# Three phase boundaries: four blocks' weights made ahead, the statistics in another PSUM bank, the first half's row factors and outputs handled inside the next group of products

## The chip, the cores and the metric

The kernel runs on one core of one Trainium2 chip. Its time is device microseconds (us) of that core; every time below is from profiles and timed runs of this kernel on such a chip. Four engines do the work and have a queue each, in which they go through their instructions in order: PE (TensorE, matrix products, with its weight loads listed apart as PEld), DVE (VectorE), ACT (ScalarE) and POOL (GpSimd). SP (SyncE) issues the loads from HBM.

## The reference

A sequence of 512 tokens of width 1024 goes through two layers, and each is a mixing part and a feed-forward part (FFN). All parts have the same frame:

```
h = h + rmsnorm(part(rmsnorm(h, pre gain)), post gain)
```

- Layer A mixes by a gated MLP (chunks of 128 tokens, six groups) beside attention to a memory of 256 rows.
- Layer B mixes by causal attention with forget gates (12 heads) beside the same kind of memory attention.
- FFN: `down(silu(x @ w_gate) * (x @ w_up))` with 2816 hidden columns, which are 22 blocks of 128.

Everything is fp32. A normalization needs, for each token, the sum of the squares of its 1024 values, that is across the whole width.

## The kernel before

**Numbers.** Each fp32 operand is split into a high part and a rest (`split`, L241): ACT writes the high part, rounded to the matrix engine's type fp32r, and DVE subtracts it from the operand to get the rest. In the profile these are `whi` and `wlo` for weights, `xshi` and `xslo` for inputs, `fhi` and `flo` for the FFN's hidden values. A product is three matmuls (`mm3`): hi by hi (L193), rest of the input by hi (L194), hi by rest of the weight (L195). One weight block, 1024 x 128 values in a tile of 128 x 1024, takes two ACT casts and two DVE subtractions of 128x512 each.

**Layout.** The residual `h` lies transposed, width on the 128 partitions and tokens along the row; the last product of a part (`y`, "out" or "down") lies the other way, tokens on the partitions, in four blocks of 128 tokens.

**A boundary** between two parts (`boundary`, L875) is called three times: from layer A's mixing to its FFN (about 140 to 195 us), from that FFN to layer B (about 500 to 550 us), and from layer B's mixing to its FFN (about 727 to 785 us). `scaled` is given in the first and third and is `None` in the second. It goes so:

1. `tail(0)` to `tail(3)`: the last products of the part before, one block of 128 tokens each. DVE adds them up into `y` (L808), ACT sums the squares (L811), DVE and POOL make the row factor `r` (L813, L262), ACT scales `y` by it (L832).
2. In between, the first four weight blocks of the next part are prepared: `block(n, aside)` issues the load and the split. For the FFN the four are gate, up, gate, up. `aside` takes the two parts from another pool (the pool of the inputs, 36 buffers) than the weights' own pool of eight pairs. `behind(...)` sets the preparation behind the last split of `tail(0)`.
3. `turn(half, pairs)`: PE transposes `y` into a PSUM bank with the tag "tr" (`yt`, L839), DVE adds it to the residual `h` (L844), ACT scales by the gain of the next norm and the result is split into `xshi` and `xslo`; ACT squares `h` (L318) and DVE adds the squares up (L321, L323). The first half of the tokens is turned before the products, the second half inside them.
4. `group(ws, inputs(0), ...)`: the products of the four blocks with the first half of the tokens (256 columns), k from 0 to 7. The fourth block begins three steps later. What stands in `after` is put behind step k: the turns of the second half behind k=3 and k=5, the norm's `finish` behind k=6.
5. `finish` (L284 on): PE sums the squares across the partitions (`st`, four one-column matmuls of which each token block takes two, L290), DVE adds epsilon (`var`, L293), POOL takes the power -1/2 (`r`, L262). `spread`: PE spreads the factors `r` over the partitions (`rb`, two transposes, L259) and DVE copies them to `rbc` (L306). The products are of unnormalized inputs; the factors come in afterwards.
6. `evac`: in the FFN, gate times `rbc` (`gr`, L1070), silu on ACT (L1072), times up (`f`, L1074), and the split into `fhi` and `flo`. This frees the four banks of the first group.
7. The same four blocks with the second half, in two groups of two, then `finish` and later `spread` and `evac` for that half.

PSUM has eight banks here: three with the tag "mm", three "lg", two "tr". The first group holds two "mm" and two "lg"; "tr" serves the transposes `yt`, the statistics `st` and the spread rows `rb`.

**Order.** The program is written in the order above, but a scheduler at build time orders the instructions of each engine by priority (the order of the text, unless `high_priority` is set) and its own estimate of when their inputs are ready, and deals out the buffers of a pool in turn. So a change in the text moves instructions in other places too.

Of the kernel before, what the change touches and what calls it, by code (L numbers as in the profile page):

```python
# [15 lines left out]
P = 128  # L16
T = 512
D = 1024
KT = 8
# [21 lines left out]
def hybrid(ctx: ExitStack, tc: tile.TileContext, i: dict, out: bass.AP):  # L41
# [12 lines left out]
    def name(s):  # L54
        n_of[s] = n_of.get(s, 0) + 1
        return f"{s}_{n_of[s]}"

    def act(s, dt=F32R, shape=(P, T)):
        return ap.tile(list(shape), dt, tag="a", name=name(s))

    def plain(s, shape=(P, T), dt=F32):
        return yp.tile(list(shape), dt, tag="y", name=name(s))
# [7 lines left out]
    def small(s, n=4, dt=F32):  # L70
        return sp.tile([P, n], dt, tag=f"s{n}", name=name(s))

    def ps(tag, shape=(P, T), s="ps"):
        return pp.tile(list(shape), F32, tag=tag, name=name(s), bufs=2 if tag == "tr" else 3)
# [26 lines left out]
    def gain(block, k):  # L101
        c = block * KT + k
        return gains[:, c : c + 1]
# [87 lines left out]
    def mm3(o, w, x, start, stop, more=False):  # L191

        PE.matmul(o, w[0], x[0], start=start, stop=False, skip_group_check=more)  # L193
        PE.matmul(o, w[0], x[1], start=False, stop=False, skip_group_check=more)  # L194
        return PE.matmul(o, w[1], x[0], start=False, stop=stop, skip_group_check=more)  # L195

    def group(ws, xs, cols, tags, nk=KT, what="ps", after={}, lag=0):


        c0, c1 = cols  # L200
        outs = [ps(t, (P, c1 - c0), s=what) for t in tags]

        def step(b, k):
            mm3(outs[b], ws[b][k], (xs[k][0][:, c0:c1], xs[k][1][:, c0:c1]), k == 0, k == nk - 1)

        last = len(ws) - 1
        for k in range(nk):
            for b in range(last):
                step(b, k)
            for x in range(0 if k == lag else k, k + 1) if k >= lag else ():  # L210
                step(last, x)
            if k in after:
                after[k]()
        return outs
# [33 lines left out]
    @contextmanager  # L248
    def behind(some):

        with ExitStack() as s:
            for ins in some:
                s.enter_context(tc.issue_after(ins.ins))
            yield
# [6 lines left out]
    def rsqrt(dst, src, n):  # L261
        G.tensor_tensor(out=dst, in0=src, in1=mhalf[:, :n], op=ALU.pow)  # L262

    class Norm:
# [13 lines left out]
                A.activation(sq, src, AF.Square)  # L278
                V.tensor_add(self.acc, self.acc, sq)

        def finish(self, cols):

            c0, c1 = cols
            tbs = range(c0 // P, c1 // P)  # L284
            t0, t1 = c0 // P, c1 // P
            st = ps("tr", (P, 4), s="st")
            for tb in tbs:
                some = self.sums(tb, cols)
                for n, sq in enumerate(some):
                    PE.matmul(st[:, tb : tb + 1], sq, avg, start=n == 0, stop=n == len(some) - 1)  # L290
            v = small("var")
            with tc.high_priority():
                V.tensor_scalar_add(v[:, t0:t1], st[:, t0:t1], RMS_EPS)  # L293
                rsqrt(self.r4[:, t0:t1], v[:, t0:t1], t1 - t0)
# [37 lines left out]
    def normed_parts(block, k, cols, hi, lo):  # L332
        c0, c1 = cols
        scaled_parts(h[:, k, c0:c1], gain(block, k), hi[:, c0:c1], lo[:, c0:c1])

    def parts(s):
        return [(act(f"{s}hi"), act(f"{s}lo")) for _ in range(KT)]
# [498 lines left out]
    def turned(ys, k, tbs, out):  # L836

        for n, tb in enumerate(tbs):
            PE.transpose(out[:, n * P : (n + 1) * P], ys[tb][k // 4][:, k % 4 * P : (k % 4 + 1) * P], ident)  # L839

    def residual(o, k, cols, post):

        c0, c1 = cols
        V.scalar_tensor_tensor(out=h[:, k, c0:c1], in0=o, scalar=gain(post, k), in1=h[:, k, c0:c1],  # L844
                               op0=ALU.mult, op1=ALU.add)
# [29 lines left out]
    def boundary(phase, post, pre, nnorm, dst, block, evac, scaled=None):  # L875

        tail, ys = phase
        h0, h1 = HALVES
        xs = {} if scaled is not None else parts("xs")

        def turn(half, pairs):
            cols = HALVES[half]
            c0, c1 = cols
            for j in pairs:
                tr = ps("tr", s="yt")
                for x in range(2):  # L890
                    turned(ys, 2 * j + x, (2 * half, 2 * half + 1), tr[:, 256 * x : 256 * x + 256])
                for x in range(2):
                    residual(tr[:, 256 * x : 256 * x + 256], 2 * j + x, cols, post)
                    if scaled is None:
                        normed_parts(pre, 2 * j + x, cols, *xs[2 * j + x])
                if scaled is not None:
                    scaled[j, half] = plain("hs", (P, 2, 256))
                    for x in range(2):
                        A.activation(scaled[j, half][:, x, :], h[:, 2 * j + x, c0:c1], AF.Copy,
                                     scale=gain(pre, 2 * j + x))  # L900
                    xs[j, half] = pair_parts("xs", scaled[j, half])
                nnorm.pair(j, cols)

        def inputs(half):
            if scaled is not None:
                return [tuple(t[:, k % 2, :] for t in xs[k // 2, half]) for k in range(KT)]
            c0, c1 = HALVES[half]
            return [tuple(t[:, c0:c1] for t in xs[k]) for k in range(KT)]

        tail(0)  # L910
        phase_parts = tuple(last_parts)
        tail(1)
        with behind(phase_parts):
            ws = [block(n, n == 2) for n in range(3)]
        tail(2)
        turn(0, range(2))
        tail(3, lambda: turn(0, (2,)))
        turn(0, (3,))
        ws.append(block(3, False))
        outs = group(ws, inputs(0), h0, ["mm", "lg"] * 2, lag=3,  # L920
                     after={3: lambda: turn(1, range(2)), 5: lambda: turn(1, range(2, 4)),
                            6: lambda: nnorm.finish(h0)})
        nnorm.spread(h0, dst)
        evac(outs, h0)
        outs = group(ws[:2], inputs(1), h0, ["mm", "lg"])
        nnorm.finish(h1)
        outs += group(ws[2:], inputs(1), h0, ["mm", "lg"])

        def close():
            nnorm.spread(h1, dst)  # L930
            evac(outs, h1)

        return xs, close

    def pair_parts(s, src, room=None):

        hi, lo = room or [act(f"{s}{n}", shape=(P, 2, 256)) for n in ("hi", "lo")]
        split(src, hi, lo)
        return hi, lo
# [120 lines left out]
    def feed_forward(layer, phase, xp, meanwhile=None):  # L1060
# [39 lines left out]

        scaled = {}
        a, close = boundary(phase, G_MIX_POST + layer, G_FFN_PRE + layer, nnorm, rb, first, evac_first, scaled)
        w = [down_weights(layer, 0, dh) for dh in range(2)]
        close()
# [42 lines left out]
    def layer_b(phase, fp):  # L1147
# [16 lines left out]
        def evac_first(outs, cols):  # L1164
            for m, o in zip(first, outs):
                queries(m, o, cols)

        a, close = boundary(phase, G_FFN_POST, G_MIX_PRE + 1, bnorm, rbc,
                            lambda n, aside: prepared(i["w_b_q"][first[n]], (KT, P), aside), evac_first)
        for m in range(2, 6):  # L1170
# [176 lines left out]
    def give(tb, order, queues=(nc.sync,)):  # L1347

        c = (tb * P, (tb + 1) * P)
        for n, some in enumerate(order):  # L1350
            tr = ps("tr", s="yt")
            for x, k in enumerate(some):
                turned(ys, k, (tb,), tr[:, x * P : (x + 1) * P])
            for x, k in enumerate(some):
                residual(tr[:, x * P : (x + 1) * P], k, c, G_FFN_POST + 1)
            k0, k1 = some[0], some[-1] + 1
            queues[n % len(queues)].dma_start(out[:, k0:k1, c[0] : c[1]], h[:, k0:k1, c[0] : c[1]])
# [69 lines left out]
```

## Time and profile before

| | us |
|---|---|
| median of 3 runs | 1115.33 (1115.09 to 1115.86) |
| the profiled execution | 1114.41 |
| its span | 1112.7 |
| PE busy / PEld busy | 1103.1 / 1000.2 |
| DVE busy / ACT busy / POOL busy | 891.2 / 660.5 / 25.4 |

The profiled execution took 0.92 us less than the median. The clock granted to PE was 0.999 of full speed over the whole span. Matmuls are pipelined, and a matmul's end is modelled: one of 256 columns is listed with 0.28 us, while the next one begins about 0.12 us after its start. So PE appears busy in pauses that are shorter than this overlap, and a pause is better read from the starts of two neighbouring matmuls. DVE and ACT instructions are listed with their own ends, which lie a little behind the start of the next.

### The profile page before, as it was taken

The numbers are of one execution on the slowest core, as the hardware profiler recorded it, in microseconds if no ns is written. First come the engines' busy times: TensorE is split into PE (matmuls) and PEld (weight loads), VectorE is DVE, ScalarE is ACT, GpSimd is POOL, SyncE is SP. The second block draws the span as 40 slices with busy tenths as digits, with TensorE's granted clock in tenths as the row PEclk, the third lists the DMA queues.
The fourth block names the chain that finished last, engine by engine and source line by source line (L and its number), as shares of the span: only waits on it lengthen the run. The fifth ranks groups of instructions, "written<-read, shape, count | busy, mean of one in ns | idle before, by whom it ended". The sixth has DMA issues, their size and how long they took to land.

```text
span 1112.7 us, 19537 instructions
## 1 busy us (share of the span) xinstructions
PE 1103.1 (99%) x7409; PEld 1000.2 (90%) x7409; DVE 891.2 (80%) x1721; ACT 660.5 (59%) x1388; POOL 25.4 (2%) x41
## 2 busy tenths in 40 slices
PE   9999999999999999999999999999999999999998
PEld 6998889999899899998988888889999899899996
DVE  7879558998698588797968889858998598588776
ACT  7775468665265254477647667768665266255453
POOL 0000000000000000001000000000000000000000
PEclk9999999999999999999999999999999999999999
DMA  7522231334134233244232654431125234233222
GB/s 268 159 79 74 88 104 58 114 95 153 57 115 136 58 111 114 77 153 151 78 95 71 159 125 130 129 95 57 58 95 161 67 109 132 65 112 116 77 76 76
DMA packets 63557, 118.12 MB, mean 106 GB/s; under 512 B 5164, under 2 KB 39992, under 8 KB 63464
## 3 DMA queue, kind: packets, MB, share of 16 engines
q1 hardware_dynamic: 62584, 116.05, 34.5%
q8 instruction: 58, 0.95, 0.4%
q0 software_dynamic: 192, 0.52, 0.2%
q10 hardware_dynamic: 688, 0.31, 0.1%
q14 instruction: 35, 0.29, 0.1%
HBM read 104.71 MB, written 2.10 MB: 96 GB/s over the span
## 4 chain that ended last, share of the span: by engine, by line
PE 89%; DVE 5%; ACT 3%; issue 1%; DMA 1%; POOL 0%; SPq 0%; POOLq 0%; DVEq 0%; ACTq 0%
PE y L193 9%; PE y L195 9%; PE y L194 9%; PE a L195 5%; PE a L193 5%; PE a L194 5%; PE e L193 3%; PE e L195 3%; PE x L193 3%; PE x L195 3%; PE e L194 3%; PE x L194 3%; PE ps L195 3%; PE ps L193 3%; PE ps L194 3%; PE v L193 2%
## 5 line engine op out<-in xcount | busy, mean ns | idle before, releaser
L241 ACT CAST whi<-raw 128x512 fp32r<-128x512 f32 x460 | 276.1, 620 | 261.3 <-PE y L195 118.6
L241 DVE TENSOR_TENSOR wlo<-raw,whi 128x512 fp32r<-128x512 f32 x460 | 305.8, 685 | 112.4 <-ACT whi L241 110.0
L193 PE MATMUL y<-whi,fhi 128*128 128x512 f32 (+1 forms) x356 | 139.8, 393 | 0.0
L194 PE MATMUL y<-wlo,fhi 128*128 128x512 f32 (+1 forms) x356 | 139.3, 391 | 0.0
L195 PE MATMUL y<-whi,flo 128*128 128x512 f32 (+1 forms) x356 | 139.3, 391 | 0.0
L193 PE MATMUL x<-xshi,whi 128*128 128x256 f32 x320 | 89.7, 280 | 0.0
L195 PE MATMUL x<-xshi,wlo 128*128 128x256 f32 x320 | 89.7, 280 | 0.0
L195 PE MATMUL a<-xshi,wlo 128*128 128x256 f32 x320 | 89.6, 281 | 0.0
L193 PE MATMUL a<-xshi,whi 128*128 128x256 f32 x320 | 89.6, 280 | 0.0
L194 PE MATMUL x<-xslo,whi 128*128 128x256 f32 x320 | 89.6, 280 | 0.0
L194 PE MATMUL a<-xslo,whi 128*128 128x256 f32 x320 | 89.5, 280 | 0.0
L195 PEld LDWEIGHTS y<-whi,flo 128*128 128x128 f32 x356 | 66.9, 188 | 15.6 <-DVE flo L241 0.2
L193 PEld LDWEIGHTS y<-whi,fhi 128*128 128x128 f32 x356 | 66.8, 188 | 15.0 <-DVE y L808 0.2
L194 PEld LDWEIGHTS y<-wlo,fhi 128*128 128x128 f32 x356 | 66.9, 188 | 14.9 <-DVE wlo L241 0.2
L195 PE MATMUL ps<-xshi,wlo 128*128 128x256 f32 (+1 forms) x224 | 66.7, 299 | 1.3 <-DVE wlo L241 1.3
L193 PE MATMUL ps<-xshi,whi 128*128 128x256 f32 (+1 forms) x224 | 67.7, 303 | 0.0
L194 PE MATMUL ps<-xslo,whi 128*128 128x256 f32 (+1 forms) x224 | 66.5, 297 | 0.0
L194 PEld LDWEIGHTS a<-xslo,whi 128*128 128x128 f32 x320 | 60.3, 188 | 0.3
L193 PEld LDWEIGHTS a<-xshi,whi 128*128 128x128 f32 x320 | 60.3, 188 | 0.3
L195 PEld LDWEIGHTS x<-xshi,wlo 128*128 128x128 f32 x320 | 60.3, 189 | 0.0
L193 PEld LDWEIGHTS x<-xshi,whi 128*128 128x128 f32 x320 | 60.3, 188 | 0.0
L194 PEld LDWEIGHTS x<-xslo,whi 128*128 128x128 f32 x320 | 60.3, 188 | 0.0
(291 smaller groups left out, 3086.7 us busy)
## 6 DMA issues: line engine op xcount, KB each, us to landing
raw<-in_w_gate SPq DMA_DIRECT2D x44, 512.0 KB
raw<-in_w_up SPq DMA_DIRECT2D x44, 512.0 KB
raw<-in_w_down SPq DMA_DIRECT2D x44, 512.0 KB
raw<-in_w_out SPq DMA_DIRECT2D x16, 512.0 KB
raw<-in_w_b_q SPq DMA_DIRECT2D x8, 512.0 KB
raw<-in_w_a_v SPq DMA_DIRECT2D x6, 512.0 KB
raw<-in_w_a_u SPq DMA_DIRECT2D x6, 512.0 KB
raw<-in_w_v SPq DMA_DIRECT2D x6, 512.0 KB
```

The costliest lines, as they stand in the source:

```text
L193: PE.matmul(o, w[0], x[0], start=start, stop=False, skip_group_check=more)
L194: PE.matmul(o, w[0], x[1], start=False, stop=False, skip_group_check=more)
L195: return PE.matmul(o, w[1], x[0], start=False, stop=stop, skip_group_check=more)
L241: last_parts[:] = A.copy(hi, src), (eng or V).tensor_sub(lo, src, hi)
```

## The change

It edits `boundary` in four ways.

1. All four weight blocks are prepared together behind the splits of `tail(0)`, and the third and the fourth are put aside. Before, only the third was, and the fourth was prepared after `tail(3)`.
2. For `scaled=None` (the second boundary) the input buffers `xs` are taken one by one in `turn(0, ...)`, and no longer all at the start.
3. `finish` for the first half uses the third "mm" bank for `st`, and no longer a "tr" bank.
4. `spread` and `evac` of the first half are put inside the next group, behind its step k=1, and no longer ahead of that group.

```diff
-        def finish(self, cols):
+        def finish(self, cols, bank="tr"):
...
-            st = ps("tr", (P, 4), s="st")
+            st = ps(bank, (P, 4), s="st")
...
-        xs = {} if scaled is not None else parts("xs")
+        xs = {} if scaled is not None else [None] * KT
...
                 for x in range(2):
+                    if scaled is None and half == 0:
+                        xs[2 * j + x] = act("xshi"), act("xslo")
                     residual(tr[:, 256 * x : 256 * x + 256], 2 * j + x, cols, post)
...
-            ws = [block(n, n == 2) for n in range(3)]
+            ws = [block(n, n >= 2) for n in range(4)]
         tail(2)
         turn(0, range(2))
         tail(3, lambda: turn(0, (2,)))
         turn(0, (3,))
-        ws.append(block(3, False))
         outs = group(ws, inputs(0), h0, ["mm", "lg"] * 2, lag=3,
                      after={3: lambda: turn(1, range(2)), 5: lambda: turn(1, range(2, 4)),
-                            6: lambda: nnorm.finish(h0)})
-        nnorm.spread(h0, dst)
-        evac(outs, h0)
-        outs = group(ws[:2], inputs(1), h0, ["mm", "lg"])
+                            6: lambda: nnorm.finish(h0, "mm")})
+
+        def give(done):
+            nnorm.spread(h0, dst)
+            evac(done, h0)
+
+        outs = group(ws[:2], inputs(1), h0, ["mm", "lg"], after={1: lambda done=outs: give(done)})
         nnorm.finish(h1)
         outs += group(ws[2:], inputs(1), h0, ["mm", "lg"])
```

As built, each engine runs the same instructions, as many as before; the orders of SP and POOL are the same, those of PE, ACT and DVE are not. The rows below are of the first boundary. A number behind a name is a buffer; the numbers differ between the two programs.

PE at the end of the first group, before. `st` stands ahead of the group's very last matmul, and `rb` behind five matmuls of the second group:

```order
L193 MATMUL ps_2057<-xshi_2036,whi_2050 128x256
L194 MATMUL ps_2057<-xslo_2037,whi_2050 128x256
L290 MATMUL st_2210<-avg,sq_1954 128x1 x2
L195 MATMUL ps_2057<-xshi_2036,wlo_2051 128x256
L193 MATMUL ps_2248<-xshi_2116,whi_1876 128x256
L194 MATMUL ps_2248<-xslo_2117,whi_1876 128x256
L195 MATMUL ps_2248<-xshi_2116,wlo_1877 128x256
L193 MATMUL ps_2249<-xshi_2116,whi_1886 128x256
L194 MATMUL ps_2249<-xslo_2117,whi_1886 128x256
L259 MATMUL rb_2228<-ident,r_3_1757 128x128 x2
L195 MATMUL ps_2249<-xshi_2116,wlo_1887 128x256
```

PE after the change, in two places. `st` stands right behind step k=6, with the 12 matmuls of k=7 after it:

```order
L193 MATMUL ps_2057<-xshi_2046,whi_1910 128x256
L194 MATMUL ps_2057<-xslo_2047,whi_1910 128x256
L195 MATMUL ps_2057<-xshi_2046,wlo_1911 128x256
L290 MATMUL st_2210<-avg,sq_1964 128x1 x2
L193 MATMUL ps_2054<-xshi_2046,whi_1880 128x256
L194 MATMUL ps_2054<-xslo_2047,whi_1880 128x256
```

And `rb` stands behind 12 matmuls of the second group:

```order
L193 MATMUL ps_2229<-xshi_2116,whi_1886 128x256
L194 MATMUL ps_2229<-xslo_2117,whi_1886 128x256
L195 MATMUL ps_2229<-xshi_2116,wlo_1887 128x256
L259 MATMUL rb_2242<-ident,r_3_1757 128x128 x2
L193 MATMUL ps_2228<-xshi_2132,whi_1876 128x256
```

So `st` moved up by 11 matmuls, and `rb` down by seven of the second group.

ACT during `tail(0)` (`raw` is a loaded weight, `whi` its high part), before:

```order
L241 CAST whi_1896<-raw_1894 128x512
L241 CAST whi_1900<-raw_1894 128x512
L811 ACTIVATE sq_1816,ss_1751<-y_1581 128x512
L811 ACTIVATE sq_1832,ss_1751<-y_1682 128x512
```

And after:

```order
L241 CAST whi_1896<-raw_1894 128x512
L241 CAST whi_1900<-raw_1894 128x512
L241 CAST whi_1906<-raw_1904 128x512
L241 CAST whi_1910<-raw_1904 128x512
L811 ACTIVATE sq_1816,ss_1751<-y_1581 128x512
```

The two casts of the fourth block stand ahead of the first sum of squares of `tail(0)`. Their two subtractions stand on DVE between the two `y` of that block. The places that they had, late in the tail, are taken by casts and subtractions of the FFN's down weights.

DVE around `var`, before:

```order
L321 TENSOR_TENSOR sq_2120<-sq_2120,sq_2136 128x512
L241 TENSOR_TENSOR xslo_2133<-hs_2129,xshi_2132 128x512
L844 SCALAR_TENSOR_TENSOR h<-yt_2163,gains,h 128x256
L844 SCALAR_TENSOR_TENSOR h<-yt_2180,gains,h 128x256
L293 TENSOR_SCALAR var_2213<-st_2210 128x2
```

And after:

```order
L321 TENSOR_TENSOR sq_2120<-sq_2120,sq_2136 128x512
L241 TENSOR_TENSOR xslo_2133<-hs_2129,xshi_2132 128x512
L293 TENSOR_SCALAR var_2213<-st_2210 128x2
L844 SCALAR_TENSOR_TENSOR h<-yt_2163,gains,h 128x256
L844 SCALAR_TENSOR_TENSOR h<-yt_2180,gains,h 128x256 x2
L241 TENSOR_TENSOR wlo_2371<-raw_2364,whi_2370 128x512
```

`var` stands two `h` further forward. The fourth block's last subtraction, which before stood on DVE some ten instructions ahead of these rows (behind the last addition of squares of the first half), is gone from there.

DVE where the first pair of blocks is evacuated (`hs` are the sums and differences that the FFN's later blocks use), after the change:

```order
L1074 TENSOR_TENSOR gr_2246<-ps_2054,rbc 128x256
L953 TENSOR_TENSOR hs_1957<-hs_1957,hs_2113 128x512
L953 TENSOR_TENSOR hs_1973<-hs_1973,hs_2129 128x512
L954 TENSOR_TENSOR hs_2113<-hs_2170,hs_2113 128x512
L954 TENSOR_TENSOR hs_2129<-hs_2187,hs_2129 128x512
L293 TENSOR_SCALAR var_2301<-st_2298 128x2
L1078 TENSOR_TENSOR f_2250<-ps_2055,silu_2248 128x256
```

Before, two subtractions of down weights and one `hs` stood between `gr` (L1070 there) and that `var`; now four `hs` do.

## Prediction

> **What bounds the kernel now.** I read the page's busy times first, then the table of PE's waits, then windows of 5 us over the boundaries, then the timeline of each engine there. The busy times:
>
> ```profile
> span 1112.7 us, 19537 instructions
> PE 1103.1 (99%) x7409; PEld 1000.2 (90%) x7409; DVE 891.2 (80%) x1721; ACT 660.5 (59%) x1388; POOL 25.4 (2%) x41
> ```
>
> PE is the bound, and only what shortens PE's own sequence or its pauses can show. The change takes no instruction away, so its worth is at most PE's pauses inside the boundaries. PE's waits there (total us, times, longest):
>
> ```profile
> PE ps L195 <- DVE wlo L241: 1.3, 2, 0.6
> PE rb L259 <- POOL r L262: 0.6, 2, 0.3
> PE st L290 <- DVE h L844: 0.3, 2, 0.2
> ```
>
> Two boundaries wait for `wlo` and for `r`, two for `h`. These figures leave out what a listed matmul's modelled end hides, so I take the pauses from starts. The first boundary's PE rows:
>
> ```profile
> 175.38 0.28 PE L194 MATMUL ps<-xslo,whi 128*128 128x256 f32 x1
> 176.28 0.38 PE L195 MATMUL ps<-xshi,wlo 128*128 128x256 f32 x1 [0.61 <-DVE wlo L241]
> 176.50 0.28 PE L193 MATMUL ps<-xshi,whi 128*128 128x256 f32 x1
> ...
> 178.71 0.37 PE L193 MATMUL ps<-xshi,whi 128*128 128x256 f32 x1
> 178.91 0.28 PE L194 MATMUL ps<-xslo,whi 128*128 128x256 f32 x1
> ...
> 181.38 0.27 PE L194 MATMUL ps<-xslo,whi 128*128 128x256 f32 x1
> 181.80 0.58 PE L290 MATMUL st<-avg,sq 128*128 128x1 f32 x4
> 182.23 0.36 PE L195 MATMUL ps<-xshi,wlo 128*128 128x256 f32 x1
> 182.44 0.28 PE L193 MATMUL ps<-xshi,whi 128*128 128x256 f32 x1
> ...
> 182.91 0.28 PE L194 MATMUL ps<-xslo,whi 128*128 128x256 f32 x1
> 183.50 0.43 PE L259 MATMUL rb<-ident,r 128*128 128x128 f32 x2 [0.31 <-POOL r L262]
> ```
>
> From 178.91 to 181.38 lie 21 matmuls without a pause, so one start follows the other by 2.47/21 = 0.118. The pause at `wlo` is 176.28 - 175.38 - 0.12 = 0.78, and the start after it is 0.10 late (0.22). At `st` it is 181.80 - 181.38 - 0.12 = 0.30, at `rb` 183.50 - 182.91 - 0.12 = 0.47. **Sum for the first boundary: 0.78 + 0.10 + 0.30 + 0.47 = 1.65.**
>
> The windows bear this out by another column (busy us of PE, then PEld, DVE, ACT, POOL with counts; granted clock; DMA):
>
> ```profile
> 175.00:180.00 5.00, 4.38 (x38) 4.18 (x37) 5.00 (x12) 4.38 (x10) 0.00 (x0) 1.00 0.35 106
> 180.00:185.00 5.00, 4.55 (x38) 4.18 (x37) 4.63 (x10) 4.16 (x9) 0.70 (x1) 1.00 0.38 107
> 185.00:190.00 5.00, 5.00 (x44) 5.00 (x44) 4.37 (x11) 4.10 (x8) 0.36 (x1) 1.00 0.15 37
> 540.00:545.00 5.00, 4.84 (x42) 4.67 (x41) 4.60 (x12) 3.32 (x8) 0.81 (x1) 1.00 0.23 89
> 760.00:765.00 5.00, 4.36 (x38) 4.16 (x37) 5.00 (x11) 4.38 (x10) 0.00 (x0) 1.00 0.33 97
> 765.00:770.00 5.00, 4.56 (x37) 4.19 (x37) 4.63 (x10) 4.17 (x10) 0.70 (x1) 1.00 0.36 116
> ```
>
> Weight loads fill an undisturbed window (5.00 in 185 to 190). They miss 0.82 + 0.82 = 1.64 in the first boundary, 0.84 + 0.81 = 1.65 in the third, and 0.33 in the second, where only `st` waits. **All three: 1.65 + 0.33 + 1.65 = 3.63.**
>
> By the matmul column the same windows miss 0.62 + 0.45 + 0.16 + 0.64 + 0.44 = 2.31. The Trainium skill's page "Perfetto Trace Analysis", section "Identifying the Most-Contended Engine", says that matmul busy time misjudges PE because matmuls are pipelined, and that weight-load busy time is better; this trace agrees, since the starts give 1.65 where the weight loads miss 1.64 and the matmuls only 1.07. By the matmul column the forecast below would be 1.3 us later.
>
> **The change part by part.** I follow the first boundary; the third, by the windows, is its copy 585 us later.
>
> *The fourth block early.* Its last subtraction stands on DVE as follows, beside the other DVE rows used below:
>
> ```profile
> 175.54 0.69 DVE L241 TENSOR_TENSOR wlo<-raw,whi 128x512 fp32r<-128x512 f32 x1
> 176.14 1.65 DVE L844 SCALAR_TENSOR_TENSOR h<-yt,gains,h 128x256 f32<-128x256 f32 x4
> ...
> 180.57 0.69 DVE L241 TENSOR_TENSOR xslo<-hs,xshi 128x512 fp32r<-128x512 f32 x1
> 181.17 0.87 DVE L844 SCALAR_TENSOR_TENSOR h<-yt,gains,h 128x256 f32<-128x256 f32 x2
> 182.41 0.16 DVE L293 TENSOR_SCALAR var<-st 128x2 f32<-128x2 f32 x1 [0.37 <-PE st L290]
> ...
> 186.55 0.42 DVE L1070 TENSOR_TENSOR gr<-ps,rbc 128x256 f32<-128x256 f32 x1
> ...
> 188.09 0.68 DVE L950 TENSOR_TENSOR hs<-hs,hs 128x512 f32<-128x512 f32 x1
> ...
> 189.47 0.42 DVE L1074 TENSOR_TENSOR f<-ps,silu 128x256 f32<-128x256 f32 x1
> ```
>
> With `wlo` made some 27 us before, PE's 0.88 is gone, and DVE is 0.60 (from 180.57 to the next start at 181.17) earlier behind it. The two casts and two subtractions move into the first tail:
>
> ```profile
> 144.40 1.66 ACT L241 CAST whi<-raw 128x512 fp32r<-128x512 f32 x3
> 147.59 0.63 ACT L811 ACTIVATE sq<-y 128x512 bf16<-128x512 f32 x1 [1.52 <-DVE y L808]
> ```
>
> ```profile
> 149.44 0.69 DVE L808 TENSOR_TENSOR y<-y,y 128x512 f32<-128x512 f32 x1 [1.89 <-PE y L195]
> ```
>
> Two casts take 2 x 0.55 = 1.1 of ACT's 1.52 idle, two subtractions 2 x 0.60 + 0.09 = 1.29 of DVE's 1.89. So they cost nothing there. The tightest place is the second boundary:
>
> ```profile
> 516.47 0.63 ACT L811 ACTIVATE sq<-y 128x512 bf16<-128x512 f32 x1 [1.06 <-DVE y L808]
> 518.11 1.34 ACT L832 ACTIVATE y<-y,r 128x512 f32<-128x512 f32 x2 [0.92 <-POOL r L262]
> ```
>
> ```profile
> 521.09 1.04 PE L839 MATMUL yt<-ident,y 128*128 128x128 f32 x8
> ```
>
> 1.1 of casts in 1.06 of idle; and if they overrun, `y` is scaled by 519.45 and transposed at 521.09: 1.64 of cover. The work that now fills the fourth block's old places (down weights) is wanted only by the next products of the FFN, so it delays nothing that PE asks for here. No load moves: SP's order is the same. Taking `xs` one by one costs no instruction; its buffers only become bound later, and I count it as 0, with the rival C for the case that a buffer is late.
>
> *`st` in another bank, 11 matmuls earlier.* With 0.88 taken off, step k=6 starts at 178.71 - 0.88 = 177.83, its 12 matmuls end at 177.83 + 0.20 + 11 x 0.118 = 179.33, and `st` can start there: by the table it waited for nothing but `h`, which had to free the "tr" bank, and the new bank is not one of those. The 0.30 go. The four small matmuls and the slower start behind them (182.23 - 181.80 = 0.43, then 0.09 more) are paid as before. k=7 then ends and group two begins at 179.33 + 0.43 + 0.20 + 11 x 0.118 = 181.26.
>
> What is new: `st` holds an "mm" bank that group two needs, so `var` must have read it by 181.26. On DVE `var` now stands behind `xslo` (180.57, now 179.97, done 180.57): it runs from 180.57 to 180.73, 0.5 ahead. If DVE had not moved forward it would be done at 181.33, a pause of 0.1. Bounds: 0 to 0.1 for each boundary.
>
> *`rb` and the outputs inside group two.* `rb` starts 12 matmuls into it, at 181.26 + 0.20 + 11 x 0.118 = 182.76. POOL's power:
>
> ```profile
> 182.74 0.70 POOL L262 TENSOR_TENSOR r<-var,mhalf 128x2 f32<-128x2 f32 x1 [11.47 <-ACT sq L318]
> ```
>
> It began 0.17 after `var` ended (182.57) and took 0.70: now 180.73 + 0.17 + 0.70 = 181.60, 1.2 ahead of `rb`. The 0.47 go, with no bound near.
>
> The outputs are later in the program, and this is the narrowest place. The fourth block's second half needs a bank that `f` frees; its first matmul stands behind `st` of the second half and 11 matmuls of the third block. Before:
>
> ```profile
> 188.86 0.50 PE L290 MATMUL st<-avg,sq 128*128 128x1 f32 x4
> ...
> 190.62 0.28 PE L193 MATMUL ps<-xshi,whi 128*128 128x256 f32 x1
> ```
>
> 1.65 earlier: 190.62 - 1.65 = 188.97. On DVE `gr` came 4.14 after `var`; two more `h` of 0.41 now lie between, so 180.57 + 4.14 + 0.82 = 185.53. Behind it 0.34 for `gr` itself and four `hs` of 0.60 (listed with 0.68, with the same overlap as `xslo`) give 188.27, then 0.08 for the second half's `var` (its `st` is done 1.65 earlier than in the trace, by 187.8), and `f` runs from 188.35 to 188.77: 0.2 ahead. If DVE had not moved forward, `f` would end at 189.37, a pause of 0.4.
>
> Sum: 3.63 gained, less 0.1 for each of the two FFN boundaries, between the 0 of my walk and the 0.5 of a DVE that has not moved (0.1 at `var`, 0.4 at `f`); I take the lower side because the 0.60 is a row that leaves DVE's own busy stretch (5.00 of 5 in 175 to 180). Gain 3.4. **The profiled execution goes from 1114.41 to 1111.0, its span to 1109.3; it lay 0.92 below the median, so the median goes to 1111.9.**
>
> **The rivals.**
>
> *B: DVE becomes the boundaries' limit.* `var`, `gr` and `f` are all on DVE, and four `hs` now stand ahead of `f`. For it: DVE is busy 5.00, 4.63 and 4.37 of 5 in the three windows. If `var` keeps its old time for lack of its inputs (done 182.57), group two waits 1.3 for the bank and `f` 0.3 more: 1.6 come back at each FFN boundary, which leaves the second's 0.33: 1115.0. If only DVE's 0.60 fails to come, it is 2 x 0.5: 1112.7. Against: DVE idled 0.37 ahead of `var` for PE alone, and this is what moves.
>
> *C: slower, ACT stands still in the tail.* The fourth block's casts are ahead of the first `sq`; ACT goes in order, so a load or a put-aside buffer that is late holds up `sq`, `r`, the scaled `y` and the transposes. The price begins beyond the 1.64 of cover, at all three boundaries: 3 us late gives 3 x 1.4 = 4.2, so 1116.1; slower than before from 2.8 us late, by over 0.2% from 3.5. Against: the load
>
> ```profile
> 141.61 0.33 SPq L154 DMA_DIRECT2D raw<-in_w_up  x1
> ```
>
> is issued 4.4 ahead of ACT's gap at 146.0, and its order on the queue has not changed.
>
> *D: the change doesn't do what it says,* another pause taking the place of each, as when the down weights' casts, now in the fourth block's slots, slip behind the silu: then only the 0.88 of `wlo` at two boundaries comes in, 1113.6. The rows of the new order speak against it.
>
> **How the numbers follow.** A 0.68, B 0.20 (half of it near 1112.7, half near 1115.0), C 0.06, D 0.06. A's own range is 1111.2 to 1112.9: all of 3.63 and another 0.5 for pauses that the matmul records hide, down to 0.5 lost at each FFN boundary and some spread. The range asked for reaches into B and D: 1111.0 to 1114.3. A measurement of this kernel tells about 0.2%, 2.2 us, from no change, so faster is below 1113.1 and slower above 1117.6. Faster: A's 0.65 and half of B, 0.74 in all; slower: half of C and a little for what I have not seen, 0.05; same 0.21.
>
> **What would show it.** Right: PE's waits list no `wlo`, `rb` or `st` row from these boundaries; weight loads are at 4.95 or more in the windows of 175 to 185 and 760 to 770; `st` has no idle ahead of it and `var` ends before group two's first matmul. B would show as `ps` L193 waiting for DVE `var` or `f` within the first matmuls of groups two and three. C would show as `sq` L811 or `whi` waiting for a load and `yt` waiting for ACT. It would be wrong if these pauses are gone and the time has not moved by 2 us: then PE pays them elsewhere.

## The result, and the profile after

| | before | after |
|---|---|---|
| median of 13 runs each, us | 1115.78 | 1113.04 (1112.66 to 1113.98) |
| ratio, 95% interval | | 0.9974 (0.9967 to 0.9982) |
| span of the profiled execution | 1112.7 | 1111.3 |

The change makes the kernel 2.7 us faster, 0.26%. The forecast was 1111.9 and its range, 1111.0 to 1114.3, held the time. The three pauses went as forecast, and more fully: the boundaries became 3.80 us shorter. But about 1.9 us of that was lost again between the boundaries, in the two FFNs, of which the forecast does not speak.

The two profiled executions are only 1.37 us apart (1114.41 and 1113.04). The changed kernel's profiled execution is just its median; that of the kernel before lay 1.37 below its median of 13. So one half of the 2.7 between the medians is seen in the traces. The other half is that most executions of the kernel before take longer than its profiled one (1114.61 to 1117.80); what makes them longer is not shown.

PE's waits after the change (total us, times, longest) have no row for `wlo` (L241), `rb` (L259) or `st` (L290) any more:

```profile
PE idle L88 <- DVE zeros L80: 1.3, 1, 1.3
PE yt L839 <- DVE y L827: 0.4, 1, 0.4
PE yt L839 <- DVE h L844: 0.4, 2, 0.2
```

The windows that showed the pauses before (busy us of PE, PEld, DVE, ACT, POOL; clock; DMA) are full, by the weight loads too:

```profile
175.00:180.00 5.00, 5.00 (x45) 5.00 (x45) 5.00 (x12) 4.98 (x11) 0.00 (x0) 1.00 0.13 25
180.00:185.00 5.00, 5.00 (x44) 5.00 (x44) 4.98 (x11) 4.09 (x10) 0.70 (x1) 1.00 0.40 125
540.00:545.00 5.00, 5.00 (x44) 5.00 (x44) 4.17 (x11) 3.02 (x7) 0.81 (x1) 1.00 0.19 70
760.00:765.00 5.00, 5.00 (x45) 5.00 (x44) 5.00 (x12) 4.97 (x12) 0.00 (x0) 1.00 0.20 55
765.00:770.00 5.00, 5.00 (x45) 5.00 (x44) 4.98 (x12) 4.10 (x10) 0.70 (x1) 1.00 0.39 122
```

The first boundary, instruction by instruction. This execution comes to the boundary 0.38 later than the one before (its first `yt` is at 160.68, not 160.30), so 0.38 is to be taken off each time when it is held against the prediction's.

```profile
179.63 0.28 PE L195 MATMUL ps<-xshi,wlo 128*128 128x256 f32 x1
179.75 0.50 PE L290 MATMUL st<-avg,sq 128*128 128x1 f32 x4
180.11 0.37 PE L193 MATMUL ps<-xshi,whi 128*128 128x256 f32 x1
...
181.63 0.28 PE L193 MATMUL ps<-xshi,whi 128*128 128x256 f32 x1
...
182.91 0.28 PE L195 MATMUL ps<-xshi,wlo 128*128 128x256 f32 x1
183.03 0.38 PE L259 MATMUL rb<-ident,r 128*128 128x128 f32 x2
...
189.15 0.28 PE L194 MATMUL ps<-xslo,whi 128*128 128x256 f32 x1
189.27 0.38 PE L193 MATMUL ps<-xshi,whi 128*128 128x256 f32 x1
189.49 0.28 PE L194 MATMUL ps<-xslo,whi 128*128 128x256 f32 x1
```

```profile
180.95 0.15 DVE L293 TENSOR_SCALAR var<-st 128x2 f32<-128x2 f32 x1
...
185.99 0.42 DVE L1074 TENSOR_TENSOR gr<-ps,rbc 128x256 f32<-128x256 f32 x1
...
188.79 0.41 DVE L1078 TENSOR_TENSOR f<-ps,silu 128x256 f32<-128x256 f32 x1
```

```profile
181.27 0.70 POOL L262 TENSOR_TENSOR r<-var,mhalf 128x2 f32<-128x2 f32 x1 [9.63 <-DVE var L293]
```

`st` starts 0.12 after the matmul ahead of it, `rb` too: no pause. Group two begins at 181.63, 0.53 after `var` has given its bank free (181.10). `f` ends at 189.20, and the fourth block's first matmul starts at 189.27, with the next one 0.22 behind it and not 0.12: this place is touched by 0.1.

Where the gain went can be read from the same two instructions in both traces, the `st` that ends a boundary and the first `yt` of the next one. Before:

```profile
188.86 0.50 PE L290 MATMUL st<-avg,sq 128*128 128x1 f32 x4
...
521.09 1.04 PE L839 MATMUL yt<-ident,y 128*128 128x128 f32 x8
...
774.75 0.50 PE L290 MATMUL st<-avg,sq 128*128 128x1 f32 x4
...
1091.10 1.03 PE L839 MATMUL yt<-ident,y 128*128 128x128 f32 x8
```

After:

```profile
187.51 0.50 PE L290 MATMUL st<-avg,sq 128*128 128x1 f32 x4
...
520.65 1.03 PE L839 MATMUL yt<-ident,y 128*128 128x128 f32 x8
...
772.12 0.50 PE L290 MATMUL st<-avg,sq 128*128 128x1 f32 x4
...
1089.76 1.03 PE L839 MATMUL yt<-ident,y 128*128 128x128 f32 x8
```

From first `yt` to last `st` the three boundaries are shorter by 1.72, 0.36 and 1.72, in all 3.80. But the stretch from 188.86 to 521.09 (332.23) now takes 333.14, and that from 774.75 to 1091.10 (316.35) takes 317.64: 0.9 and 1.3 more, with the same instructions and next to no pause. PE's matmuls simply follow each other more slowly there. In the second FFN, for one, the mean start-to-start time of the 256-column matmuls between 800 and 1085 us is 118.56 ns, where it was 117.73 ns (some 1,600 of them in each trace; 0.83 x 1,600 = 1.3 us; starts more than 0.14 us apart are left out of these means). This accounts for the profiled gain: 3.80 less 0.9 and 1.3, less the 0.38 by which this execution came later to the first boundary, and with 0.1 gained in layer B between the second and the third, makes 1.3; 1.37 were measured.

### The profile page after: what moved, and what is told of

Same layout as the page of the kernel before. It is cut to its first block, busy times and chain, and to the rows that moved or that the text cites. A ratio compares the mean times of both kernels' runs of the same rounds, so it can differ in the third digit from the quotient of the medians.

```text
span 1111.3 us, 19551 instructions
## 1 busy us (share of the span) xinstructions
PE 1103.8 (99%) x7408; PEld 1002.1 (90%) x7409; DVE 890.6 (80%) x1721; ACT 663.0 (60%) x1388; POOL 25.2 (2%) x41
## 2 busy tenths in 40 slices
DMA packets 63557, 118.12 MB, mean 106 GB/s; under 512 B 5164, under 2 KB 39992, under 8 KB 63464
## 4 chain that ended last, share of the span: by engine, by line
PE 94%; DVE 2%; ACT 1%; DMA 1%; issue 1%; SPq 0%; POOLq 0%; POOL 0%; DVEq 0%; ACTq 0%
PE y L193 10%; PE y L194 10%; PE y L195 10%; PE a L194 5%; PE a L195 5%; PE a L193 5%; PE ps L193 4%; PE ps L194 4%; PE ps L195 4%; PE e L193 3%; PE x L195 3%; PE x L194 3%; PE e L195 3%; PE e L194 3%; PE x L193 3%; PE v L193 2%
## 5 line engine op out<-in xcount | busy, mean ns | idle before, releaser
L241 ACT CAST whi<-raw 128x512 fp32r<-128x512 f32 x460 | 277.4, 620 | 264.2 <-PE y L195 118.5
L241 DVE TENSOR_TENSOR wlo<-raw,whi 128x512 fp32r<-128x512 f32 x460 | 306.8, 688 | 116.8 <-ACT whi L241 114.4
```

Source lines behind the costliest of these rows:

```text
L241: last_parts[:] = A.copy(hi, src), (eng or V).tensor_sub(lo, src, hi)
```

## The experiments

Two questions: does each edit remove its own pause, and what slows the FFN between the boundaries? Pauses are taken from the starts of neighbouring matmuls, as in the prediction; "boundaries" are the lengths from first `yt` to last `st`, against the kernel before.

### Each kernel once more

> The kernel before, unchanged, profiled a second time, to learn how far two profiles of one kernel agree away from the boundaries. The pauses at wlo, st and rb should come back within 0.1 of 0.88, 0.30 and 0.47 at the first boundary, as they follow from the order. Theory (the 2.3 us that the changed kernel's profile lost between the boundaries is chance): the mean start-to-start time of 256-column matmuls in 200 to 350 us, 0.1176 in the first profile, comes out anywhere from 0.1175 to 0.1186. Rival (the change slows the FFN's blocks): it is 0.1174 to 0.1179 here and 0.1182 to 0.1188 in every profile of the changed kernel.

Measured: 1116.03, ratio to the kernel before 1.0003 (0.9995 to 1.0012). The boundaries agree with the first profile within 0.01, and so does the second FFN: 117.74 ns, 316.28 us. What does vary is the first FFN, 0.60 longer than in the first profile (PE pauses for 0.42 and 0.10 at 262 us, waiting for ACT), and the start of the program, 0.39 longer.

> The changed kernel, unchanged, profiled a second time. No pause at wlo, st or rb; 0.1 at the fourth block's first matmul, as in the first profile. Theory (chance): the mean start-to-start time of 256-column matmuls in 200 to 350 us moves from its 0.1184 by 0.0003 or more, either way. Rival (the change slows the FFN's blocks): 0.1182 to 0.1188 again in 200 to 350, 800 to 930 and 960 to 1085 us. Timed: 0.997 to 0.998 of the kernel before.

Measured: 1113.11, ratio 0.9979 (0.9970 to 0.9988). The boundaries are shorter by 1.72, 0.36 and 1.72 again, and the second FFN runs at 118.55 ns. So the slower pace of the second FFN is no chance: the second execution of each kernel came within 0.01 ns of the first, and the change moves it by 0.83. The first FFN is slower too, by more than chance. Over 200 to 350 us the pace is 117.57 and 117.63 ns in the two executions of the kernel before and 118.18 and 118.12 ns in those of the changed one; between 300 and 350 us, where no execution has a gap, it is 117.30 and 117.21 against 118.27 and 118.29. With the pauses of single executions taken out, the first FFN takes about 332.3 us before and 332.9 after: 0.6 of the 0.9 belong to the change. So the rival of both expectations holds, the change slows the FFN's blocks, though the 118.1 and 118.2 ns of 200 to 350 us lie at the lower edge of its 0.1182 to 0.1188. The two profiled executions here are 1.84 us apart (1115.29 and 1113.45).

### One edit alone

Fourth block early, with `xs` taken one by one (parts 1 and 2 of the change; the lines on `xs` are left out here):

```diff
-            ws = [block(n, n == 2) for n in range(3)]
+            ws = [block(n, n >= 2) for n in range(4)]
...
-        ws.append(block(3, False))
```

> The kernel before with the fourth block prepared early (and xs taken one by one) alone. Theory (three pauses, each with its own edit): at the first and third boundary wlo's 0.88 go, st keeps 0.30 and rb 0.47. Rival (one chain through DVE): PE comes to st 0.88 earlier, DVE with the h that frees the bank only 0.60 earlier, so st waits 0.5 to 0.6, and the edit is worth 0.6 of its 0.88. Pace in the second FFN (mean start-to-start of 256-column matmuls in 960 to 1085 us): 118.4 to 118.7 ns as in the changed kernel if the fourth block's new buffers set it, 117.7 if not.

The trace around `st` (PE) and the work that it waits for (DVE):

```profile
181.90 0.58 PE L290 MATMUL st<-avg,sq 128*128 128x1 f32 x4 [0.94 <-DVE h L844]
```

```profile
181.28 0.87 DVE L844 SCALAR_TENSOR_TENSOR h<-yt,gains,h 128x256 f32<-128x256 f32 x2
182.51 0.16 DVE L293 TENSOR_SCALAR var<-st 128x2 f32<-128x2 f32 x1 [0.37 <-PE st L290]
```

`wlo`'s pause is gone, but `st` now waits 1.10 (and 1.16 at the third boundary), `rb` 0.47 and 0.44 as before. The first boundary is 0.02 shorter, the second 0.02 longer, so the edit alone is worth nothing. The mechanism is the rival's: PE arrives earlier at an `h` that DVE has not finished. `st` begins 20.89 after the boundary's first `yt`, where it was 21.50, so it did gain DVE's 0.6. But the scheduler also set `st` forward in this program: 56 matmuls lie between it and the `st` of the second half, where 51 did. Five matmuls (0.59) that PE had done ahead of `st` now wait behind it, and they take back what the rival had counted as the edit's worth. What the edit earns with `st` in its old place was not run. (The third boundary cannot be compared in length, since PE's granted clock, the figure ahead of the last two in this row, was 0.66 there.)

```profile
770.00:775.00 5.00, 4.98 (x29) 4.98 (x30) 5.00 (x11) 2.23 (x6) 0.00 (x0) 0.66 0.35 105
```

`st` in an "mm" bank, nothing else:

```diff
-            st = ps("tr", (P, 4), s="st")
+            st = ps(bank, (P, 4), s="st")
...
-                            6: lambda: nnorm.finish(h0)})
+                            6: lambda: nnorm.finish(h0, "mm")})
```

> The kernel before with st in an mm bank alone. Theory (three pauses, each with its own edit): st's 0.30 go, wlo's 0.88 and rb's 0.47 stay at the first and third boundary, and the second loses its 0.33: 0.9 us in all. Rival (one chain through DVE and POOL): var comes earlier with st, so rb's pause shrinks to 0.1 too: 1.7 us in all.

```profile
177.54 0.39 PE L195 MATMUL ps<-xshi,wlo 128*128 128x256 f32 x1 [0.61 <-DVE wlo L241]
...
181.46 0.50 PE L290 MATMUL st<-avg,sq 128*128 128x1 f32 x4
...
183.37 0.43 PE L259 MATMUL rb<-ident,r 128*128 128x128 f32 x2
```

`wlo` is waited for as before; neither `st` nor `rb` is. The boundaries are 0.80, 0.37 and 0.45 shorter, 1.62 in all: the rival again. (At the third, `wlo`'s pause was 1.13 here and also with the next edit, not 0.80; in both, DVE's queue shows 0.24 of "issue" ahead of an `xslo`, with nothing that it waits for. Why is open.)

Row factors and outputs inside group two, nothing else:

> The kernel before with the first half's row factors and outputs behind step k=1 of the second group alone. Both theories: wlo's 0.88 and st's 0.30 stay at the first and third boundary and rb's 0.47 go, since rb now stands behind 12 matmuls of the second group (1.4 us) and r is ready 1.2 after the pause at st: 0.9 us in all. If the pause moves again, as it did from wlo to st with the fourth block alone, it shows at the third or fourth block of the second half, by 0.2 to 0.5. Pace in the second FFN as in the kernel before, 117.7 ns.

```profile
176.44 0.39 PE L195 MATMUL ps<-xshi,wlo 128*128 128x256 f32 x1 [0.61 <-DVE wlo L241]
...
181.96 0.58 PE L290 MATMUL st<-avg,sq 128*128 128x1 f32 x4
...
183.89 0.28 PE L195 MATMUL ps<-xshi,wlo 128*128 128x256 f32 x1
184.01 0.38 PE L259 MATMUL rb<-ident,r 128*128 128x128 f32 x2
```

Measured: `wlo` 0.77 + 0.11 and `st` 0.27 stay, `rb`'s pause is gone, nothing new appears. The first boundary is 0.53 shorter, the second the same, the third 0.16 (with `wlo`'s 1.13). Pace 117.73 ns. As expected.

### Two edits, without the last

> The change without its last part: the first half's row factors and outputs stand ahead of the second group again, so that rb comes between the two groups. Theory (part four earns its own 0.4): in the changed kernel's trace r is ready at 181.97 and the second group begins at 181.63, so rb waits 0.3 to 0.5 at the first and third boundary and the kernel is 0.6 to 1.0 us slower than the changed one. Rival (st ahead by 11 matmuls brings r early enough by itself): no pause at rb above 0.1, the same time as the changed kernel within 0.3 us.

```profile
182.01 0.28 PE L195 MATMUL ps<-xshi,wlo 128*128 128x256 f32 x1
182.52 0.43 PE L259 MATMUL rb<-ident,r 128*128 128x128 f32 x2 [0.23 <-POOL r L262]
```

`rb` waits 0.39 and 0.42; 1114.32, ratio 0.9987 (0.9978 to 0.9996), 1.2 us above the changed kernel on the same chip, where 0.6 to 1.0 were expected; 0.94 of it are at the boundaries. So part four does earn its 0.4 here. With `st` moved and `wlo`'s pause left in (`st` alone) `rb` did not wait, and there it would have had nothing to earn.

| edits | boundaries, us | in all |
|---|---|---|
| fourth block early, `xs` | -0.02, +0.02, not comparable | about 0 |
| `st` in "mm" | -0.80, -0.37, -0.45 | -1.62 |
| outputs in group two | -0.53, 0.00, -0.16 | -0.69 |
| first two | -1.27, -0.35, -1.24 | -2.86 |
| all three | -1.72, -0.36, -1.72 | -3.80 |

The single edits add up to 2.3, together they bring 3.8. Part of this gap is the third boundary, where none of the three single runs is clean (the clock in one, `wlo`'s longer pause in two). At the first boundary, where all are, they add up to 1.35 and together bring 1.72.

The single edits were executed once each: 1118.34 (block), 1115.97 (`st`) and 1114.17 (outputs), with the kernel before at medians of 1115.77, 1115.40 and 1116.33 on the same chips. These times hold more than the edit: the first took 1.5 us more at the third boundary, the second came 1.3 later to the first boundary and took 1.6 more in the first FFN. So only lengths within the trace are compared.

### How narrow the place at `f` is

```diff
-        outs = group(ws[:2], inputs(1), h0, ["mm", "lg"], after={1: lambda done=outs: give(done)})
+        outs = group(ws[:2], inputs(1), h0, ["mm", "lg"], after={5: lambda done=outs: give(done)})
```

> The changed kernel with the first half's row factors and outputs behind step k=5 of the second group, not k=1. Theory (f is the narrow place: 0.07 between its end and the fourth block's first matmul): rb 2.8 us later makes f end near 190.4 where the fourth block, four matmuls further back in this order, could start at 189.7, a pause of 0.5 to 0.8 at the first and third boundary. Rival (the place has room, the 0.1 seen there is only a slower start): no pause above 0.2.

```profile
187.36 0.50 PE L290 MATMUL st<-avg,sq 128*128 128x1 f32 x4
187.97 0.39 PE L193 MATMUL ps<-xshi,whi 128*128 128x256 f32 x1
188.19 0.28 PE L194 MATMUL ps<-xslo,whi 128*128 128x256 f32 x1
```

```profile
187.50 0.41 DVE L1074 TENSOR_TENSOR gr<-ps,rbc 128x256 f32<-128x256 f32 x1
```

There is a pause, 0.25 + 0.10 (0.28 + 0.10 at the third boundary), but at the third block's first matmul, which needs the bank that `gr` frees (187.91), not at the fourth's. `f` ends at 190.12 and no pause of over 0.06 follows. So neither expectation fits: the place has no room to spare, but `gr` is late ahead of `f`.

### What slows the FFN

All the kernels so far that put the fourth block aside run the second FFN at 118.55 to 118.57 ns and 300 to 350 us of the first at 118.3, and all that don't at 117.73 to 117.75 and 117.2 to 117.3. The block's edit alone is enough for it (`xs` comes with that edit, but only behind the first FFN). The instructions from 300 to 350 us and from 965 to 1080 us stand in the same order on every engine in both. What differs is where buffers lie: the fourth block no longer takes from the weights' pool but from that of the inputs, so later weights and inputs get other slots. The first idea was the distance between the high part and the rest of a weight piece, since in the second FFN they come from other pairs of slots. In the first FFN they are the same distance apart in both programs, so there the distance cannot be what slows it. To test the idea in the second, both parts in one tile, side by side:

```diff
-        return (wp.tile([P, max(n, 512)], F32R, tag="hi", name=name("whi"), bufs=8)[:, :n],
-                wp.tile([P, max(n, 512)], F32R, tag="lo", name=name("wlo"), bufs=8)[:, :n])
+        both = wp.tile([P, 2, max(n, 512)], F32R, tag="hilo", name=name("w"), bufs=8)
+        return both[:, 0, :n], both[:, 1, :n]
```

in the kernel before and in the changed one:

> The kernel before, with the high part and the rest of each weight piece in one tile, side by side, so that their distance is the same for every piece whatever was put where earlier. Theory (the pace of the second FFN hangs on where the two parts of a weight lie to each other): the mean start-to-start of 256-column matmuls in 960 to 1085 us is within 0.2 ns of that of the changed kernel with the same edit, both somewhere between 117 and 119. Rival (something else that the change moves sets it): 0.8 ns apart, 117.75 here and 118.58 there. The pauses at the boundaries are those of the kernel before.

> The changed kernel with the same edit (both parts of each weight piece side by side in one tile). Theory (where the parts lie sets the pace): pace in 960 to 1085 us within 0.2 ns of the kernel before with this edit, and this kernel 3.4 to 4.0 us faster than that one, the whole sum of the pauses. Rival: 0.8 ns slower than that one in 960 to 1085 us, and 2.0 to 2.8 us faster in all, as without the edit.

Then two kernels with exactly the changed kernel's order on every engine. The one takes the two buffers in the other order, so that high parts and rests change places:

> The changed kernel with the two buffers of a weight piece taken in the other order (rest first, then high part), so that the two pools lie the other way round in memory and the pairs of buffers differ; the order of the instructions is the same on every engine. Theory (where the parts of the weights lie sets PE's pace): in 960 to 1085 us the mean start-to-start of 256-column matmuls leaves 118.58 ns by 0.3 or more, either way. Rival (the order of ACT's and DVE's work set it, which the side-by-side edit also moved): 118.5 to 118.65 again. Boundary pauses as in the changed kernel (none but the 0.1).

The other makes each rest's buffer 64 bytes longer:

> The changed kernel with 64 bytes more in each buffer of a weight's rest, so that these buffers move by 0 to 448 bytes against everything else; nothing else, and the same order on every engine. Theory (places of the weight parts): 0.1 to 0.8 off 118.58 ns in 960 to 1085 us; if only coarse distances count, it stays and after_swap moves. Rival (order): 118.5 to 118.65 in both.

And the side-by-side kernel with the rest first:

> The changed kernel with both parts of a weight piece side by side, rest first and high part second; the same order on every engine as with the high part first. Theory (places): the pace in 960 to 1085 us leaves the 117.18 ns of that kernel by 0.2 or more. Rival (the other order of ACT and DVE that the shared tile brings is what made it fast): 117.1 to 117.3 again, and the same 1109.9 us within 0.6.

The ratios are to the kernel before on the same chip; the first row is the first comparison's.

| kernel | median, us | ratio to before | 256-column matmuls, ns, 800 to 1085 us | second FFN, `st` to `yt`, us |
|---|---|---|---|---|
| before | 1115.78 | | 117.73 | 316.35 |
| after | 1113.04 | 0.9974 (0.9967 to 0.9982) | 118.56 | 317.64 |
| after_swap | 1113.03 | 0.9972 (0.9961 to 0.9982) | 118.56 | 317.67 |
| after_lo16 | 1114.27 | 0.9981 (0.9973 to 0.9990) | 118.80 | 318.25 |
| before_adj | 1115.01 | 0.9992 (0.9983 to 1.0001) | 117.29 | 315.69 |
| after_adj | 1109.90 | 0.9949 (0.9935 to 0.9962) | 117.13 | 315.38 |
| adj_swap | 1109.39 | 0.9940 (0.9928 to 0.9953) | 117.14 | 315.38 |

The second FFN of the kernel with longer rests, and of the changed one with both parts side by side:

```profile
772.77 0.50 PE L290 MATMUL st<-avg,sq 128*128 128x1 f32 x4
...
1091.02 0.71 PE L839 MATMUL yt<-ident,y 128*128 128x128 f32 x5
```

```profile
770.85 0.50 PE L290 MATMUL st<-avg,sq 128*128 128x1 f32 x4
...
1086.23 1.03 PE L839 MATMUL yt<-ident,y 128*128 128x128 f32 x8
```

With both parts side by side the changed kernel is no longer slower there than the one before (315.38 against 315.69), and it is 5.1 us faster in all, 4.1 of it at the boundaries; 3.4 to 4.0 were expected. But the two do not run alike. Over 800 to 930 us their means agree (117.08 both), in 960 to 1085 us they differ by 0.54 ns (117.18 and 117.72), and between 300 and 350 us by 1.4 ns (116.77 and 118.16), with the same order of instructions in both and every pair side by side. So "within 0.2" failed, and the distance between a piece's parts is not what sets the pace, or not alone.

Exchanging the two parts changed nothing, in either form, against the expectation. Making the rests' buffers longer, in the same order of instructions, changed the pace by 0.24 ns, as expected, and in 380 to 500 us from 117.5 to 118.2 ns. (It moves the rests by 0 to 448 bytes and also the buffers that lie behind them, some of the FFN's inputs among them, by 512.) So the places of buffers alone do move PE's pace. Which places count, those of weights or of inputs, and to what, is open. The side-by-side tile also changes ACT's and DVE's order in the FFN and that of a few instructions on PE and SP, so how much of its gain is the place and how much the order is open too, as is what on the chip makes a matmul 1 ns slower.

The changed kernel with both parts side by side beats both the kernel before and the change: 1109.4 to 1109.9, 0.5 to 0.6% under the kernel before. The kernel before with the same edit stays where it was (0.9992).

## Why the prediction was right, and where not

- **What bounds the kernel.** Right. PE was the limit, and of its three pauses none is left in the waits. But that the worth is "at most PE's pauses" leaves out PE's pace, which moved too, here the wrong way; with both parts of a weight side by side it moved the other way.
- **The size of the pauses.** Right, and the weight-load column was the right one: 3.63 were read, 3.80 came in. The rest is in part what a smooth `st` saves (0.36 to the next matmul, 0.43 before). The matmul column's 2.31 would have been far too little. The Trainium skill's page "Perfetto Trace Analysis", section "Identifying the Most-Contended Engine", prefers weight-load busy time to matmul busy time; the trace after agrees, with 5.00 in place of 4.18.
- **Which edit earns which term.** Right for the three together, wrong one by one. The sum credits `wlo`'s 0.88 to the early block, 0.30 to the bank, 0.47 to the outputs' place. The runs show that the waits hang together: with the block alone `st` waits 1.10 for `h` on DVE, and nothing is earned (0.59 of that wait is due to `st`'s place further forward); the bank alone takes `rb`'s pause with it. The terms add up only since all three waits were removed.
- **The walk through the boundary.** With 0.38 taken off, `st` at 179.37 (179.33 forecast), `var` 180.57 (180.57), `r` ready 181.59 (181.60), group two 181.25 (181.26), `rb` 182.65 (182.76), `f` 188.41 (188.35), fourth block 188.89 (188.97). Every step held within 0.11.
- **The charge of 0.1 for each FFN boundary.** It came true at `f`: `var` cost nothing, and the start behind `f` is 0.10 late at both. The charge was chosen between 0 and 0.5, and the walk had left 0.2 of room at `f` where 0.07 was, so that it fits to 0.1 is partly luck.
- **The cover for the early casts.** Right. At the first boundary the five casts end 0.45 before `sq` can start; at the second `y` is scaled by 519.86, 0.79 ahead of `yt` (1.64 before):

```profile
144.78 2.73 ACT L241 CAST whi<-raw 128x512 fp32r<-128x512 f32 x5
147.96 0.63 ACT L811 ACTIVATE sq<-y 128x512 bf16<-128x512 f32 x1 [0.45 <-DVE y L808]
```

```profile
518.52 1.34 ACT L832 ACTIVATE y<-y,r 128x512 f32<-128x512 f32 x2 [0.92 <-POOL r L262]
```

- **The step that failed** is the sum itself: it takes everything outside the boundaries as unchanged. "The work that now fills the fourth block's old places ... delays nothing" was true of pauses, and "its buffers only become bound later, and I count it as 0" was said of `xs`; that buffers of weights and inputs lie elsewhere once the fourth block comes from another pool was not costed at all. PE's matmuls then follow each other more slowly, for about 0.6 us in the first FFN and 1.3 in the second. 3.80 less 1.9 is 1.9, where the sum gave 3.4; the two pairs of profiled executions are 1.37 and 1.84 apart.
- **What made the number better than the sum.** The sum was for the profiled execution, 1111.0, and that came at 1113.04, 2.0 later. The forecast of the median added 0.92, as the profile before lay that far under its median of three. The changed kernel's profile lies at its median, so this step was wrong by 0.92 the other way, and the median missed by only 1.1. That is luck. 1113.04 also lies outside A's own range, 1111.2 to 1112.9; the range asked for holds it because it was widened for B and D, which did not come.
- **The rivals.** B did not come: no wait of group two for `var`, and its narrow place cost only the 0.1. C did not: at the second boundary one cast waits 0.49 for its load, as it did before the change (0.50), and nothing behind it is held up. D did not: all pauses went. The last sentence of "What would show it", that PE might pay elsewhere, is what partly happened.

## What to carry to other kernels

Pauses of one engine that wait for the same chain on another hang together: removing the first alone was worth nothing here, and the sum came only with the last. Look also where the scheduler sets the next wait after a single edit; five matmuls decided that run. Read a pause from the starts of neighbouring instructions, where the ends are modelled. And when a tile moves to another pool, compare the pace between two fixed instructions far from the edit: everything behind it may get other buffers.

## What the runs showed of the hardware that was not expected

- The mean pace of PE's 256-column matmuls in a stretch came back within 0.01 ns in a second execution of each of two kernels (117.73 and 117.74; 118.56 and 118.55), and differs between programs with the same instructions by up to 1.7 ns (117.13 to 118.80), 1.4% of a matmul. In one and the same order of instructions, 64 bytes more in each of eight buffers, with what lies behind them moved too, changed it by 0.24 ns.
- In one execution PE's granted clock was 0.66 over the 5 us from 770, right after two pauses of 1.16 and 0.44; its 256-column matmuls start 0.21 apart there from 770.6 to 773.6, and 0.12 again behind. In no other trace of this case did the clock fall at these places.
